# Where a hybrid transformer block opens the buffers of its second weight pair, and in which order the quarters of its output projection run

## The chip, the cores and the metric

The kernel runs on one core of one Trainium2 chip. The metric is the device time of one execution in microseconds (us); lower is better. Five engines run beside each other, each with its own instruction queue: TensorE (PE in the profile, its weight loads are PEld), VectorE (DVE), ScalarE (ACT), GpSimd (POOL) and SyncE (SP), which here only issues DMA loads.

## The reference

One layer for 256 tokens of width 2048, all in float32. The part that this case is about is the end of the first half and the start of the second:

```
h  = x + concat(att, u) @ w_out            # w_out: 2048 x 2048
hn = rms_norm(h, norm2_g)
a  = hn @ w_gate ; bu = hn @ w_up          # 2048 x 5632 each
h  = h + (silu(a) * bu) @ w_down           # 5632 x 2048
```

Ahead of it stand the input projection, a differential attention of 4 heads (whose output is `att`) and a causal convolution with layer norm (whose output is `u`).

## The kernel before, in words

**Precision.** Every float32 operand is split into a rounded half `hi` and a rest `lo`. A product of two split operands takes three matmuls (hi·hi, lo·hi, hi·lo). A weight chunk is loaded raw by SP, rounded to `hi` by ACT (L351) and its rest is taken by DVE (L360, `wlo<-raw,whi`). For some chunks, those written with a capital letter in `ORDER`, ACT writes −raw (L354) and POOL adds the raw weights by an accumulating DMA (L355) in place of DVE's subtraction.

**w_out.** Its 2048 columns go in four quarters of 512 (n = 0, 1, 2, 3). A chunk is two rows of 128 by 512 columns, 12 matmuls. Quarters 0, 1 and 2 go side by side: rows 0–3 of each, rows 4–5 of each, rows 6–7 of each, then rows 8–15 of each (4 chunks a quarter); quarter 3 then runs alone with all its 8 chunks. The text counts chunks back from the end of w_out: quarter 3 is chunks −8 to −1, the last four chunks of the quarter before it are −12 to −9, the ones before those −16 to −13; the very first chunk of w_out is −32. Accumulators lie in PSUM: a pair of banks of the pool `acc` (4 banks), but quarter 2 takes a pair of the pool `aux` (4 banks), which also serves every transpose and the attention's small products.

**What follows a quarter.** `out_done(n)` adds the accumulators to the residual (DVE, L874, two instructions, one for each 128 tokens), sends `h` to `out`, scales `h` (ACT, L883), transposes it on PE in two groups (L891, tile `ps_h`) and evacuates each group: quarters 0 and 2 into `hn` (ACT, L895); quarters 1 and 3 into a `hi` (ACT, L899) and a `lo` (DVE, L901). After quarter 2 it starts `make_forms`, which builds seven combinations of the blocks of `hn` (for a Strassen-like product with 7 multiplications) as hi (`fhi`, ACT L1009–L1011 and L1020) and lo (`flo`, DVE L1017, L1018, L1022), from sums by DVE (L1007, L1008, L1013, L1014).

**The second half** goes in 11 column blocks of gate and up. A block has 12 units: four `s` (a pair of rows from both matrices at once, 7 products of 3 matmuls each, Q1, Q6, Q7, Q5, Q2, Q4, Q3 in this order in the first), and eight plain chunks of gate (`g`) or up (`u`). A string gives the order; block 0 has one of its own. The weights of an `s` unit come as one load of 1 MB (`wb`); DVE makes sums of it (L1041–L1043, the "sums"), ACT rounds it (L1050, L1054, L1055, tile `wh`), and DVE takes the rests (L1059, L1060, tile `wl`); rounding and rests together are called its split below. `wh` and `wl` exist twice (`ffn["w", 0]` and `ffn["w", 1]`), for even and odd `s` units. The first set is opened after quarter 0 of w_out; the second by `open_second`, at the end of `out_done(3)`, when the whole group of pools of the first half (`h`, attention outputs, small vectors) is closed. Products Q1, Q6, Q7, Q5 take the four `acc` banks, Q2, Q4, Q3 and an eighth sum QX the four `aux` banks. At the last `s` unit of a block DVE runs six `bank_sums` (L1188–L1193), which free the banks for the next block.

**Who issues when.** The program text is emitted by one Python loop over chunks (`run_chunks`); each engine executes what it is given in that order, and waits in that order. Before it emits the matmuls of chunk t, the loop emits what looks ahead: in w_out the rest of chunk t+2 and the rounding of chunk t+3; from two chunks before the second half on, the rests of chunks up to t+3 (`LO_AHEAD`), the sums up to t+5, the roundings with a DMA up to t+5, other roundings up to t+4, loads up to t+9. Work that follows a quarter is a generator; each call of `resume()` lets each of them go one step on. `resume()` is called in the middle and at the end of a plain chunk, and in an `s` unit behind products 2, 4 and 6 and at the end. `start(done)` only queues a generator: its first step comes with the next `resume()`. A unit marked `prompt` calls `resume()` once more right behind its own last matmul.

A PSUM or SBUF tile that is asked for takes the place freed longest ago, and its first writer waits until the last reader of the old tile is done.

Of the kernel before, what the change touches and what calls it, by code (L numbers as in the profile page):

```python
# [13 lines left out]
F32 = mybir.dt.float32  # L14
# [67 lines left out]

ORDER = "sgGsgGsUUsUu"

FIRST = "sgguusGsGsUu"

Q1, Q6, Q7, Q5, Q2, Q4, Q3, QX = range(8)

PRODUCTS = ((Q1, 0, 5), (Q6, 5, 0), (Q7, 6, 1), (Q5, 4, 2), (Q2, 1, 6), (Q4, 2, 3), (Q3, 3, 4))
# [28 lines left out]
def tile_block(  # L118
# [9 lines left out]

    wp = ctx.enter_context(tc.tile_pool(name="wp", bufs=4))
    early = ctx.enter_context(tc.tile_pool(name="early", bufs=2))  # L130
    latestack, prestack = ExitStack(), ExitStack()
    vectors = latestack.enter_context(tc.tile_pool(name="vectors", bufs=1, side="right"))
    late = latestack.enter_context(tc.tile_pool(name="late", bufs=1, side="right"))
    once = latestack.enter_context(tc.tile_pool(name="once", bufs=1, side="right"))
    small = latestack.enter_context(tc.tile_pool(name="small", bufs=4, side="right"))
    pre = prestack.enter_context(tc.tile_pool(name="pre", bufs=2))
    acc_ps = ctx.enter_context(tc.tile_pool(name="acc", bufs=4, space=PSUM))
    aux_ps = ctx.enter_context(tc.tile_pool(name="aux", bufs=AUX, space=PSUM))
# [5 lines left out]
    ident = const.tile([P, P], F32, tag="ident", name="ident")  # L144
    make_identity(nc, ident)
    arena = [const.tile([P, BLOCKS, P], F32R, tag=f"l{x}", name=f"l{x}") for x in ("hi", "lo")]
    neghalf = vectors.tile([P, 8], F32, tag="neghalf", name="neghalf")
    pool.memset(neghalf, -0.5)


# [4 lines left out]

    warm_up(WARM)

    cols = vectors.tile([P, NR], F32, tag="cols", name="cols")
    halves_of_x = [early.tile([P, HK, S], F32, tag="wb", name="xt") for _ in range(2)]

    def x_load(ks, queue):
# [2 lines left out]
        queue.dma_start(out=halves_of_x[i][:, k : k + n].rearrange("p k s -> p (k s)"),  # L164
                        in_=xt[:, NR + ks[0] * S : NR + (ks[0] + n) * S])

    head = late.tile([P, NK * N], F32, tag="lod", name="head", bufs=1)[:, : NR + S]
    act.dma_start(out=head, in_=xt[:, : NR + S])
    x_load(XPARTS[1], act)
    x_load(range(2, 4), act)  # L170
    pool.tensor_scalar(cols, head[:, :NR], 1.0, 0.0, ALU.mult, ALU.add)

    act.copy(small.tile([P, 8], F32, tag="rsq", name="first"), neghalf)

    def col(key, k):
        return cols[:, AT[key] + k : AT[key] + k + 1]
# [165 lines left out]
        sp.dma_start(out=c["raw"].rearrange("p k n -> p (k n)"), in_=src)  # L342

    def minus_chunk(c):
        c["lo"] = c["view"](late.tile([P, NK * N], F32R, tag="lod", name="lod", bufs=1))
        act.activation(c["lo"], c["raw"], AF.Copy, scale=-1.0)
        pool.dma_start(out=c["lo"].rearrange("p k n -> p (k n)"), in_=c["src"].bitcast(F32R), accum_op=ALU.add)

# [134 lines left out]
    def run_chunks():  # L483
        n = len(chunks)
        pair_at.extend(i for i, c in enumerate(chunks) if "sides" in c)
        two_at.extend(i for i, c in enumerate(chunks) if "kind" in c and "sides" not in c)
        at = dict(part=0, dma=0, sums=0, round=0, minus=0, raw=0)
        first = next(i for i, c in enumerate(chunks) if "kind" in c)

        def until(what, do, stop, only=lambda c: True, may=lambda i: True):  # L490
            while at[what] < min(n, stop) and may(at[what]):
                if only(chunks[at[what]]):
                    do(at[what])
                at[what] += 1

        for t in range(n):
            if t >= first - AHEAD:
                until("part", part_of, t + 1 + LO_AHEAD)
                until("raw", lambda i: round_raw(chunks[i]), t + 1 + RAW_AHEAD, lambda c: "sides" in c,
                      lambda i: i <= t or may_round_raw(t, i))  # L500
                ahead = SUMS_AHEAD if t >= first else 0
                until("sums", sums_of, t + 1 + ahead - ("sides" in chunks[t] and bool(chunks[t].get("prompt"))), may=may_sum)
                until("dma", round_of, t + 1 + DMA_AHEAD, lambda c: c["by_dma"])
                until("round", round_of, t + 1 + (HI_AHEAD if t >= first else LO_AHEAD))
                load_until(t + 1 + LOAD_AHEAD)
            else:
                if t < len(XPARTS):
                    until("part", part_of, t + 2)
                else:
                    until("part", part_of, t + 1 + AHEAD)  # L510
                    until("minus", minus_of, min(t + 1 + MINUS_AHEAD, first), lambda c: c.get("minus"))
                    until("round", round_of, min(t + 1 + ROUND_AHEAD, first))
            part_of(t)
            chunks[t]["multiply"](chunks[t])
            if chunks[t].get("prompt") and chunks[t]["done"]:
                resume()
        while running:
            resume()
# [99 lines left out]
    def conv_back(b):  # L618
# [19 lines left out]
            return  # L638
        yield

        act.activation(small.tile([P, 8], F32, tag="rsq", name="first"), neghalf, AF.Silu)
        mv = small.tile([P, NM, 2], F32, tag="mv", name="mv", bufs=1)
        for m in range(NM):
            dve.bn_aggr(mv[:, m, :], stats[m].rearrange("p a b -> p (a b)"))
# [11 lines left out]
        for b in range(2):  # L656
            for t in range(NB // 2):
                yield from room(1)
                pt = aux_ps.tile([P, 2, S], F32, tag="aux", name="ps_ln")
                for j in range(2):  # L660
                    i = 2 * t + j
                    for m in range(NM):
                        pe.transpose(pt[:, j, m * P : (m + 1) * P], ytok[m, b][:, i * P : (i + 1) * P], ident)
                for j in range(2):
                    ct = b * NB + 2 * t + j
                    z = pre.tile([P, N], F32, tag="va", name="z")[:, :S]
                    act.activation(z, pt[:, j, :], AF.Silu, bias=col("lb", ct), scale=col("lg", ct))
                    hi = late.tile([P, S], F32R, tag="mchi", name=f"mchi{ct}", bufs=NCT)
                    lo = late.tile([P, S], F32R, tag="mclo", name=f"mclo{ct}", bufs=NCT)
                    dve.tensor_copy(hi, z)  # L670
                    dve.tensor_tensor(lo, z, hi.bitcast(F32), ALU.subtract)
                    mixc[ct] = (hi, lo)
                spend(0.7)
                yield from lag(2)
# [132 lines left out]
    def attend_values(hd):  # L807
# [26 lines left out]
        for e in range(2):  # L834
            for m in range(NM):
                pe.transpose(pt[:, e, m * P : (m + 1) * P], atts[m][:, e * P : (e + 1) * P], ident)
        pairs = [lhs_pair("a", 2 * hd + e) if hd >= 2 else tuple(
            late.tile([P, S], F32R, tag=t, name=t, bufs=4) for t in ("mahi", "malo")) for e in range(2)]
        for e, (hi, _) in enumerate(pairs):
            act.activation(hi, pt[:, e, :], AF.Copy, scale=col("sg", e))  # L840
        for e, (hi, lo) in enumerate(pairs):
# [20 lines left out]

    def open_second():

        latestack.close()
        spare_lhs.append(ffn["wt"].tile([P, SPARE, 2, S], F32R, tag="ahi", name="ahi"))
        fp = ffn["sum"] = ffn["w", 1] = ctx.enter_context(tc.tile_pool(name="ffn1", bufs=1))
        spare_lhs.append(fp.tile([P, SPARE, 2, S], F32R, tag="alo", name="alo"))
        ffn["plain"].append([fp.tile([P, HK - NS, S], F32R, tag=x, name=x) for x in ("chi", "clo")])

    def out_done(n, ps):
        cs = slice(n * N, (n + 1) * N)
        for m in range(NM):
            dve.tensor_tensor(h[m][:, cs], h[m][:, cs], ps[m], ALU.add)  # L874
        for m in range(NM):
# [33 lines left out]
        if n == D // N - 1:  # L909
            yield  # L910
            for m in range(NM):
                ss = small.tile([P, 1], F32, tag="ssh", name="ssh")
                dve.tensor_reduce(ss, ss2[m], AX.X, ALU.add)
                rsqrt_mean(rest[m], ss, D, EPS)
                pool.tensor_tensor(rest[m], rest[m], rms1[:, m : m + 1], ALU.mult)
            open_second()
            yield from lag(2)
            at = slot[0] % (KD // 2) * 4 - 2 * 4
            for a, c in zip(arena, ffn["plain"][1]):
                act.copy(c, a[:, at : at + 8].rearrange("p (k m) c -> p k (m c)", m=NM))  # L920
            for k in REST:
                i, k_ = divmod(k, HK)
                plain[k] = tuple(c[:, k_ - NS] for c in ffn["plain"][i])
# [145 lines left out]
    def multiply_pair(c):  # L1069
# [4 lines left out]
        for n, (q, f, w) in enumerate(products):  # L1074
# [3 lines left out]
            pe.matmul(ps, flo[:, f, p, :], c["hi"][:, w], start=False, stop=False)  # L1078
            pe.matmul(ps, fhi[:, f, p, :], c["lo"][:, w], start=False, stop=bool(last))  # L1079
            if n == 0 and c["done"]:  # L1080
                halfway["w1"] = ffn["sum"].tile([P, N], F32, tag="sum0", name="sum0")
                act.copy(halfway["w1"], ps)
            if n in (1, 3, 5):
# [180 lines left out]
        block("w_in", VC + b * N, range(KD), fx, lambda ps, b=b: v_done(b, ps))  # L1264
    for ks, first, last in ((range(0, 4), True, False), (range(4, 6), False, False), (range(6, 8), False, False),
                            (range(8, 16), False, True)):
        for n in range(3):
            block("w_out", n * N, ks, fm, (lambda ps, n=n: out_done(n, ps)) if last else None,
                  bkey=("o", n), first=first, last=last, spare=n == 2)
    block("w_out", 3 * N, range(16), fm, lambda ps: out_done(3, ps))  # L1270
    for m in range(NM):
        chunks[RAW_BUFS + m]["raw_tag"] = f"v{m}"
    for i, c in enumerate(chunks[len(XPARTS) : -12]):
# [2 lines left out]
    j0 = 0  # L1276
    for g, nb in enumerate(FGROUPS):
        for j in range(j0, j0 + nb):
            gate_up_block(j, FIRST if j == 0 else ORDER)
        for n in range(0, D // N, 2):  # L1280
            down_block(g, n)
        j0 += nb
# [46 lines left out]
```

## Time and profile before

| | |
|---|---|
| median of 3 runs | 1045.86 us (1045.74 to 1046.52) |
| the profiled execution | 1046.47 us, of which the span from first to last instruction is 1044.6 us |
| granted TensorE clock in it | 0.995 of full speed |
| busy share of the span | PE 98%, DVE 85%, ACT 68%, POOL 15% |
| where things lie | w_out's first chunk at about 241 us; its last matmuls at 338; block 0 of the second half 339 to 391; then ten more blocks and the down projections |

A timeline row reads: start in us, duration in us, engine, line, operation, tile written `<-` tiles read, shape, count of merged instructions, and in brackets how long the engine had been idle and what ended that. Durations of back-to-back matmuls overlap (a row says 0.39, their starts are 0.23 apart). A row of a table by stretches gives, for each engine, its busy time in the stretch and the count of its instructions, then the granted clock, the busy share of the DMA engines and GB/s. A row of waits gives total, times, longest.

### The profile page before, as it was taken

The numbers are of one execution on the slowest core, as the hardware profiler recorded it, in microseconds if no ns is written. First come the engines' busy times: TensorE is split into PE (matmuls) and PEld (weight loads), VectorE is DVE, ScalarE is ACT, GpSimd is POOL, SyncE is SP. The second block draws the span as 40 slices with busy tenths as digits, with TensorE's granted clock in tenths as the row PEclk, the third lists the DMA queues.
The fourth block names the chain that finished last, engine by engine and source line by source line (L and its number), as shares of the span: only waits on it lengthen the run. The fifth ranks groups of instructions, "written<-read, shape, count | busy, mean of one in ns | idle before, by whom it ended". The sixth has DMA issues, their size and how long they took to land. (4 is left out here: it accounts for less than half of the span.)

```text
span 1044.6 us, 13138 instructions
## 1 busy us (share of the span) xinstructions
PE 1027.8 (98%) x4621; PEld 847.4 (81%) x4621; DVE 891.6 (85%) x1121; ACT 707.6 (68%) x939; POOL 159.1 (15%) x205
## 2 busy tenths in 40 slices
PE   9999999999999798999999999999999999999998
PEld 7888888888888587888888888888888888888887
DVE  6699889897657599999999888999898897998984
ACT  7754667767766477687666666876766566767761
POOL 0140322311100111011012120110100221001121
PEclk9999999999999899999999999999999999999999
DMA  9968675665657398897989997988979999889896
GB/s 360 320 196 247 217 217 175 201 194 182 193 190 262 121 303 237 267 311 229 304 237 257 303 267 249 317 250 275 272 233 291 273 264 324 239 258 301 237 255 134
DMA packets 65346, 260.15 MB, mean 249 GB/s; under 512 B 7296, under 2 KB 8576, under 8 KB 56832
## 3 DMA queue, kind: packets, MB, share of 16 engines
q1 hardware_dynamic: 47648, 202.13, 52.9%
q0 software_dynamic: 17200, 56.63, 29.1%
q8 instruction: 36, 0.59, 0.2%
q10 hardware_dynamic: 432, 0.55, 0.2%
q14 instruction: 30, 0.25, 0.1%
HBM read 250.90 MB, written 8.39 MB: 248 GB/s over the span
## 5 line engine op out<-in xcount | busy, mean ns | idle before, releaser
L351 ACT CAST whi<-raw 128x1024 fp32r<-128x1024 f32 (+1 forms) x246 | 253.6, 1041 | 49.2 <-PE acc L391 31.8
L360 DVE TENSOR_TENSOR wlo<-raw,whi 128x1024 fp32r<-128x1024 f32 (+1 forms) x154 | 185.2, 1211 | 42.4 <-ACT whi L351 39.0
L1059 DVE TENSOR_TENSOR wl<-wb,wh 128x2048 fp32r<-128x2048 f32 x66 | 151.1, 2289 | 43.0 <-ACT wh L1054 42.6
L1050 ACT CAST wh<-wb 128x1536 fp32r<-128x1536 f32 x66 | 97.9, 1483 | 125.4 <-issue 65.8
L355 POOL DMA_DIRECT2D wlo<-in_wts_dram x78 | 68.7, 881 | 533.4 <-ACT wlo L354 409.7
L390 PE MATMUL acc<-whi,lhi 128*128 128x512 f32 x352 | 139.3, 396 | 0.2 <-ACT whi L351 0.2
L391 PE MATMUL acc<-whi,llo 128*128 128x512 f32 x352 | 137.6, 391 | 0.0
L1077 PE MATMUL q<-wh,fhi 128*128 128x512 f32 x308 | 122.0, 396 | 8.9 <-DVE h L874 6.1
L1079 PE MATMUL q<-wl,fhi 128*128 128x512 f32 x308 | 121.2, 393 | 1.4 <-DVE wl L1059 0.7
L1078 PE MATMUL q<-wh,flo 128*128 128x512 f32 x308 | 121.0, 393 | 0.0
L1060 DVE TENSOR_TENSOR wl<-wt,wh 128x1536 fp32r<-128x1536 f32 x66 | 115.7, 1752 | 0.0
L604 DVE SCALAR_TENSOR_TENSOR y<-upad,cw,y 128x256 f32<-128x256 f32 x240 | 100.8, 487 | 3.4 <-ACT y L597 3.4
L1055 ACT CAST wh<-wt 128x1536 fp32r<-128x1536 f32 x66 | 97.6, 1479 | 0.0
L1104 PE MATMUL q<-wlo,chi 128*128 128x512 f32 x336 | 91.3, 394 | 0.0
L1099 PE MATMUL q<-whi,chi 128*128 128x512 f32 x336 | 90.0, 390 | 0.0
L1099 PE MATMUL q<-whi,clo 128*128 128x512 f32 x336 | 89.9, 389 | 0.0
L396 PE MATMUL acc<-wlo,lhi 128*128 128x512 f32 x304 | 83.5, 395 | 0.6 <-DVE wlo L360 0.6
L354 ACT ACTIVATE wlo<-raw 128x1024 fp32r<-128x1024 f32 x78 | 82.3, 1055 | 0.0
L1041 DVE TENSOR_TENSOR wt<-wb 128x1024 f32<-128x1024 f32 x66 | 80.6, 1221 | 1.2 <-DMA wb<-in_wts_dram 0.7
L390 PEld LDWEIGHTS acc<-whi,lhi 128*128 128x128 f32 x352 | 66.4, 189 | 14.2 <-ACT whi L351 0.6
L391 PEld LDWEIGHTS acc<-whi,llo 128*128 128x128 f32 x352 | 66.4, 189 | 13.6
L1077 PEld LDWEIGHTS q<-wh,fhi 128*128 128x128 f32 x308 | 58.4, 190 | 22.5 <-DVE h L874 6.4
(221 smaller groups left out, 1792.8 us busy)
## 6 DMA issues: line engine op xcount, KB each, us to landing
raw<-in_wts_dram SPq DMA_DIRECT2D x242, 512.0 KB, 6.9
wb<-in_wts_dram SPq DMA_DIRECT2D x66, 1024.0 KB, 7.1
wlo<-in_wts_dram POOLq DMA_DIRECT2D x78, 512.0 KB, 9.3
lod<-in_wts_dram POOLq DMA_DIRECT2D x14, 512.0 KB, 6.1
out_dram<-sum POOLq DMA_DIRECT2D x22, 256.0 KB, 6.0
h<-in_x_dram SPq DMA_DIRECT2D x4, 512.0 KB, 8.9
out_dram<-h POOLq DMA_DIRECT2D x8, 256.0 KB, 3.5
xt<-in_xt_dram SPq DMA_DIRECT2D x6, 256.0 KB, 6.7
```

The costliest lines, as they stand in the source:

```text
L351: act.copy(c["hi"], c["raw"])
L360: dve.tensor_tensor(c["lo"], c["raw"], c["hi"].bitcast(F32), ALU.subtract)
L390: pe.matmul(ps[m], xhi[:, ms], hi[:, j, :], start=c["first"] and j == 0, stop=False)
L391: pe.matmul(ps[m], xlo[:, ms], hi[:, j, :], start=False, stop=False)
L604: dve.scalar_tensor_tensor(y[:, ct, :], src, wk, y[:, ct, :], ALU.mult, ALU.add)
L1050: act.copy(c["hi"][:, 4:], c["b"][:, 1:])
L1059: dve.tensor_tensor(c["lo"][:, 3:], c["b"], c["hi"][:, 3:].bitcast(F32), ALU.subtract)
L1060: dve.tensor_tensor(c["lo"][:, :3], c["t"], c["hi"][:, :3].bitcast(F32), ALU.subtract)
L1077: pe.matmul(ps, fhi[:, f, p, :], c["hi"][:, w], start=bool(first), stop=False)
L1078: pe.matmul(ps, flo[:, f, p, :], c["hi"][:, w], start=False, stop=False)
L1079: pe.matmul(ps, fhi[:, f, p, :], c["lo"][:, w], start=False, stop=bool(last))
L1099: pe.matmul(ps, plain[i][e][:, ms], hi[:, i, ns], stop=False, start=i == e == 0 and bool(c["first"].get(qs[m])))
```

## The change

Four things are moved.

- The pools on the right side of SBUF are regrouped. What w_out's matmuls read (attention and convolution outputs, and one weight buffer) goes into a pool `mix`, which is closed in the first step of `out_done(3)`; in its place `wh` and `wl` of the second set open there. The rest of the old group is closed where everything was closed before (now `open_third`).
- The last chunk of w_out is marked `prompt`, so the first step of `out_done(3)` is emitted right behind w_out's last matmul. In the two chunks ahead of the second half, rests are taken for one unit beyond t in place of three.
- Block 0 takes the order of the other blocks, `sgGsgGsUUsUu`, in place of `sgguusGsGsUu`. Its second `s` unit is then unit 3, not unit 5, and it has three plain chunks by DVE in place of five.
- w_out's first three quarters go 0, 2, 1 in each round, so quarter 2 ends with chunk −13 and quarter 1 with chunk −9.

The copy of two tiles at the end of `out_done(3)` comes ten steps later in place of two, and a unit that needs the pool of sums waits in the loop until it is open. A vector of constants is widened from 8 to 32 columns.

```
-FIRST = "sgguusGsGsUu"
...
-    latestack, prestack = ExitStack(), ExitStack()
-    vectors = latestack.enter_context(tc.tile_pool(name="vectors", bufs=1, side="right"))
+    latestack, mixstack, prestack = ExitStack(), ExitStack(), ExitStack()
...
+    mix = mixstack.enter_context(tc.tile_pool(name="mix", bufs=1, side="right"))
...
-                until("part", part_of, t + 1 + LO_AHEAD)
+                until("part", part_of, t + 1 + (LO_AHEAD if t >= first else 1))
...
-                    hi = late.tile([P, S], F32R, tag="mchi", name=f"mchi{ct}", bufs=NCT)
+                    hi = mix.tile([P, S], F32R, tag="mchi", name=f"mchi{ct}", bufs=NCT)
...
     def open_second():
 
+        mixstack.close()
+        ffn["w", 1] = ctx.enter_context(tc.tile_pool(name="ffn1", bufs=1))
+        for x in ("wh", "wl"):
+            ffn["w", 1].tile([P, 7, N], F32R, tag=x, name=x)
+
+    def open_third():
+
         latestack.close()
         spare_lhs.append(ffn["wt"].tile([P, SPARE, 2, S], F32R, tag="ahi", name="ahi"))
-        fp = ffn["sum"] = ffn["w", 1] = ctx.enter_context(tc.tile_pool(name="ffn1", bufs=1))
+        fp = ffn["sum"] = ctx.enter_context(tc.tile_pool(name="ffn2", bufs=1))
...
     def out_done(n, ps):
         cs = slice(n * N, (n + 1) * N)
+        if n == D // N - 1:
+            open_second()
...
-            open_second()
-            yield from lag(2)
+            open_third()
+            yield from lag(10)
...
+                while "sum" not in ffn:
+                    resume()
                 halfway["w1"] = ffn["sum"].tile([P, N], F32, tag="sum0", name="sum0")
...
-        for n in range(3):
+        for n in (0, 2, 1):
             block("w_out", n * N, ks, fm, (lambda ps, n=n: out_done(n, ps)) if last else None,
                   bkey=("o", n), first=first, last=last, spare=n == 2)
     block("w_out", 3 * N, range(16), fm, lambda ps: out_done(3, ps))
+    chunks[-1]["prompt"] = True
...
-            gate_up_block(j, FIRST if j == 0 else ORDER)
+            gate_up_block(j, ORDER)
```

More of the change, by code (lines that the diff above doesn't have):

```diff
@@ L146, in tile_block @@
     arena = [const.tile([P, BLOCKS, P], F32R, tag=f"l{x}", name=f"l{x}") for x in ("hi", "lo")]
-    neghalf = vectors.tile([P, 8], F32, tag="neghalf", name="neghalf")
+    neghalf = once.tile([P, 32], F32, tag="neghalf", name="neghalf")
     pool.memset(neghalf, -0.5)
@@ L156, in tile_block @@
     warm_up(WARM)
-    cols = vectors.tile([P, NR], F32, tag="cols", name="cols")
+    cols = once.tile([P, NR], F32, tag="cols", name="cols")
     halves_of_x = [early.tile([P, HK, S], F32, tag="wb", name="xt") for _ in range(2)]
@@ L165, in x_load @@
                         in_=xt[:, NR + ks[0] * S : NR + (ks[0] + n) * S])
-    head = late.tile([P, NK * N], F32, tag="lod", name="head", bufs=1)[:, : NR + S]
+    head = mix.tile([P, NK * N], F32, tag="lod", name="head", bufs=1)[:, : NR + S]
     act.dma_start(out=head, in_=xt[:, : NR + S])
@@ L171, in tile_block @@
     pool.tensor_scalar(cols, head[:, :NR], 1.0, 0.0, ALU.mult, ALU.add)
-    act.copy(small.tile([P, 8], F32, tag="rsq", name="first"), neghalf)
+    act.copy(small.tile([P, 8], F32, tag="rsq", name="first"), neghalf[:, :8])
     def col(key, k):
@@ L344, in minus_chunk @@
     def minus_chunk(c):
-        c["lo"] = c["view"](late.tile([P, NK * N], F32R, tag="lod", name="lod", bufs=1))
+        c["lo"] = c["view"](mix.tile([P, NK * N], F32R, tag="lod", name="lod", bufs=1))
         act.activation(c["lo"], c["raw"], AF.Copy, scale=-1.0)
@@ L639, in conv_back @@
         yield
-        act.activation(small.tile([P, 8], F32, tag="rsq", name="first"), neghalf, AF.Silu)
+        act.activation(small.tile([P, 8], F32, tag="rsq", name="first"), neghalf[:, :8], AF.Silu)
         mv = small.tile([P, NM, 2], F32, tag="mv", name="mv", bufs=1)
@@ L667, in conv_back @@
                     act.activation(z, pt[:, j, :], AF.Silu, bias=col("lb", ct), scale=col("lg", ct))
-                    hi = late.tile([P, S], F32R, tag="mchi", name=f"mchi{ct}", bufs=NCT)
-                    lo = late.tile([P, S], F32R, tag="mclo", name=f"mclo{ct}", bufs=NCT)
+                    hi = mix.tile([P, S], F32R, tag="mchi", name=f"mchi{ct}", bufs=NCT)
+                    lo = mix.tile([P, S], F32R, tag="mclo", name=f"mclo{ct}", bufs=NCT)
                     dve.tensor_copy(hi, z)
@@ L837, in attend_values @@
         pairs = [lhs_pair("a", 2 * hd + e) if hd >= 2 else tuple(
-            late.tile([P, S], F32R, tag=t, name=t, bufs=4) for t in ("mahi", "malo")) for e in range(2)]
+            mix.tile([P, S], F32R, tag=t, name=t, bufs=4) for t in ("mahi", "malo")) for e in range(2)]
         for e, (hi, _) in enumerate(pairs):
```

## The prediction

> **What bounds the kernel now.** I read the page's busy shares first, then PE's waits, then the table by stretches of 5 us where they fall.
>
> ```profile
> PE 1027.8 (98%) x4621; PEld 847.4 (81%) x4621; DVE 891.6 (85%) x1121; ACT 707.6 (68%) x939; POOL 159.1 (15%) x205
> ...
> PE q L1077 <- DVE h L874: 6.1, 1, 6.1
> PE q L1077 <- DVE sum L1188: 2.7, 1, 2.7
> ...
> PE q L1079 <- DVE wl L1059: 0.7, 1, 0.7
> PE q L1079 <- DVE wl L1060: 0.7, 1, 0.7
> ...
> 345.00:350.00 5.00, 2.24 (x5) 1.82 (x6) 3.23 (x5) 1.34 (x2) 1.09 (x2) 0.50 0.89 356
> ...
> 395.00:400.00 5.00, 5.00 (x14) 3.46 (x15) 4.90 (x9) 2.34 (x4) 0.00 (x0) 0.66 0.78 207
> ```
>
> PE is busy for 98% of the span, so only its losses are to be won, and they sit in one place: the start of the second half. Two waits there for DVE, of 6.1 and 2.7 us, and behind each a stretch at a granted clock of 0.50 and 0.66.
>
> ```profile
> 338.89 0.39 PE L1077 MATMUL q<-wh,fhi 128*128 128x512 f32 x1
> ...
> 347.76 0.79 PE L1077 MATMUL q<-wh,fhi 128*128 128x512 f32 x1 [6.09 <-DVE h L874]
> ...
> 352.79 0.60 PE L891 MATMUL ps_h<-ident,scaled 128*128 128x128 f32 x4
> 353.47 0.47 PE L1077 MATMUL q<-wh,fhi 128*128 128x512 f32 x1
> ...
> 354.23 1.07 PE L1099 MATMUL q<-whi,chi 128*128 128x512 f32 x4
> ...
> 391.31 0.39 PE L1077 MATMUL q<-wh,fhi 128*128 128x512 f32 x1
> ...
> 400.94 1.07 PE L1099 MATMUL q<-whi,chi 128*128 128x512 f32 x4
> ...
> 437.95 0.39 PE L1077 MATMUL q<-wh,fhi 128*128 128x512 f32 x1
> ...
> 442.03 0.39 PE L1077 MATMUL q<-wh,fhi 128*128 128x512 f32 x1
> ```
>
> An undisturbed `s` unit: six products from 437.95 to 442.03, 0.68 each, so 7 take 4.76. The first `s` unit runs from 338.89 to 354.23, 15.34, with two groups of transposes inside (0.36 each, estimated from a 0.60 row whose instructions overlap): 9.9 lost. The first of block 1 takes 400.94 − 391.31 = 9.63: 4.9 lost, of which 2.7 is the wait and the rest the low clock. With 0.7 at block 0's second `s` unit, **the loss before is 15.5 us**.
>
> Why PE waited 6.1 us is read on DVE.
>
> ```profile
> 341.03 3.49 DVE L360 TENSOR_TENSOR wlo<-raw,whi 128x1024 fp32r<-128x1024 f32 x3
> 344.44 1.22 DVE L1041 TENSOR_TENSOR wt<-wb 128x1024 f32<-128x1024 f32 x1
> ...
> 347.02 1.28 DVE L874 TENSOR_TENSOR h<-h,acc 128x512 f32<-128x512 f32 x2
> 352.45 0.88 DVE L901 SCALAR_TENSOR_TENSOR llo<-ps_h,cols,lhi 128x256 fp32r<-128x256 f32 x2 [4.15 <-ACT lhi L899]
> ```
>
> Quarter 3's addition L874, which frees the banks for Q7 and Q5, stood behind three rests and the next pair's sums. The last row matters for what follows: Q3 (353.47) starts 0.68 after the transposes, not 0.36, and right behind L901's end (353.33). Q3 takes the `aux` bank freed longest ago, that of the first `ps_h`, and waits until L901 has read it.
>
> **The change part by part.** Times below are on the clock of before, to be read against its rows.
>
> *Prompt, and one unit of look-ahead.* L874 of quarter 3 is now emitted before unit 0's look-ahead, with no rests of `g` units ahead of it. It can run as soon as w_out's last matmul ends: the 6.1 us go. The wide constant and the dummy tiles cost nothing on a path; POOL, which fills the constant, is 15% busy.
>
> *Opening `mix`.* `wh` and `wl` are 2 × 7 × 512 × 4 B = 28 KB a partition; `mix` holds 4 KB + 8 × 2 KB + 4 × 2 KB = 28 KB, whose last reader is w_out's last matmul. So unit 3 can be rounded at once. Before, ACT waited for the vector work behind quarter 3, and DVE stood still meanwhile.
>
> *What is late next.* Unit 0's look-ahead reaches unit 3, now an `s` unit: before its own matmuls the loop emits `g`'s rest, sums and split of unit 3, and the roundings of units 4 and 5. Quarter 3's L899 and L901 come behind all of it, and Q3 waits for L901. The pieces:
>
> ```profile
> 316.64 1.34 ACT L883 ACTIVATE scaled<-h,rstd 128x512 f32<-128x512 f32 x2
> ...
> 338.41 3.88 ACT L351 CAST whi<-raw 128x1024 fp32r<-128x1024 f32 x4
> ...
> 351.58 0.84 ACT L899 ACTIVATE lhi<-ps_h,cols 128x256 fp32r<-128x256 f32 x2 [2.50 <-PE ps_h L891]
> ...
> 315.92 1.28 DVE L874 TENSOR_TENSOR h<-h,acc 128x512 f32<-128x512 f32 x2 [0.41 <-PE acc L396]
> 317.12 1.22 DVE L360 TENSOR_TENSOR wlo<-raw,whi 128x1024 fp32r<-128x1024 f32 x1
> ...
> 333.80 1.22 DVE L1041 TENSOR_TENSOR wt<-wb 128x1024 f32<-128x1024 f32 x1
> ...
> 337.15 2.29 DVE L1059 TENSOR_TENSOR wl<-wb,wh 128x2048 fp32r<-128x2048 f32 x1 [0.69 <-ACT wh L1054]
> 339.36 1.75 DVE L1060 TENSOR_TENSOR wl<-wt,wh 128x1536 fp32r<-128x1536 f32 x1
> ```
>
> From the end E of w_out: L874 at E − 0.25, 1.20 until the next DVE instruction (315.92 to 317.12); `g`'s rest 1.15; sums 2.66 (333.80 to 337.15 − 0.69): E + 4.76. ACT then needs 1.95 for L1054 and L1055 (336.46 to 338.41), 3 × 0.95 for two roundings and one negative (the row with x4), then L899; L901 follows 0.87 behind it (351.58 to 352.45) and takes 0.88. Sum: E + 4.76 + 1.95 + 2.85 + 0.87 + 0.88 = E + 11.3, and Q3 at E + 11.4. PE has until then Q1 and Q6 (1.36), the transposes (behind L883, which ends 2.06 after L874 starts, so 0.5 late), Q7, Q5, Q2, Q4 and the second transposes: E + 5.3. It waits about 6.1 us there, and as before the low clock behind it costs 1.9 (347.76 to 352.79 holds four products and a group of transposes, 3.1 undisturbed, and took 5.0). **Unit 0 loses 0.5 + 6.1 + 1.9 = 8.5.** Bounds: 0.5 if L901 were not waited for, 10.5 if a load holds ACT up by 2. Unit 2's weights are a load of
>
> ```profile
> raw<-in_wts_dram SPq DMA_DIRECT2D x242, 512.0 KB, 6.9
> ```
>
> 6.9 us; it can be issued at about 333 (a buffer freed by chunk −3's rest), so its rounding, now ahead of `g`'s on ACT, is done by 342. I take 8.5, since the steps are rows. POOL's adding DMA for it has until 359.
>
> *Order 0, 2, 1.* `make_forms` runs four chunks earlier, so that unit 0 is split before w_out ends and its two small waits go, but the rows below now meet the work behind quarter 1.
>
> ```profile
> 312.08 1.99 ACT L351 CAST whi<-raw 128x1024 fp32r<-128x1024 f32 x2
> 324.87 0.61 ACT L1009 CAST fhi<-hn 128x512 fp32r<-128x512 f32 x1
> ...
> 326.44 1.04 ACT L351 CAST whi<-raw 128x1024 fp32r<-128x1024 f32 x1
> 328.78 1.91 ACT L1020 CAST fhi<-sums 128x2048 fp32r<-128x2048 f32 x1
> ...
> 328.65 1.29 DVE L1017 TENSOR_TENSOR flo<-hn,fhi 128x512 fp32r<-128x512 f32 x2
> 329.86 0.68 DVE L1018 SCALAR_TENSOR_TENSOR flo<-hn,fhi 128x512 fp32r<-128x512 f32 x1
> 331.59 2.29 DVE L1022 TENSOR_TENSOR flo<-sums,fhi 128x2048 fp32r<-128x2048 f32 x1
> ...
> 318.89 0.60 PE L891 MATMUL ps_h<-ident,scaled 128*128 128x128 f32 x4
> ```
>
> ACT: rounding of −7 at 312.08 to 313.0, three casts 1.57 (324.87 to 326.44) to 314.6, rounding of −6 to 315.6. DVE: rest of −6 to 316.85, L1017 and L1018 1.8 to 318.65, and only then quarter 1's L874, 2.7 later than its slot (315.92). L883 ends at 320.7, and PE, which wants to transpose at 318.89, waits 1.9. L1020 (1.9) stands between L883 and L899 on ACT: L901 starts at 323.4. From there DVE has no gap: L901 0.8, rest 1.15, L901 0.8, L1022 2.2, rest 1.15, sums 2.66, rest 1.15, L1059 2.2, L1060 1.7, rest of −2 1.2: 338.4. PE wants that rest at 336.9 (second half of −2, already 1.9 late) and waits 1.5 more. After it come 0.9 and a chunk of 2.72: w_out ends at 342.0 in place of 338.9. **3.1 lost.** Bounds: 1.9 (the transposes alone) and 4.5 (the chain's steps each 0.1 longer).
>
> Quarter 2's two `aux` banks are also taken two chunks earlier, at −30, just behind the convolution's transposes:
>
> ```profile
> 249.87 1.46 PE L817 MATMUL ps_o<-v,qT 128*128 128x256 f32 x6
> ...
> 250.36 1.09 ACT L630 COPY upad<-ps_y 128x512 f32<-128x512 f32 x2
> ```
>
> With two banks held by quarter 2, head 2's `ps_o` needs a bank of `ps_y`, free when ACT's first copy ends at 250.9. **1.1 lost**; bounds 0 (another bank is free) and 1.6 (the second copy).
>
> *Block 0's order.* Unit 3's split is done at E + 9.3, well before PE asks for it; DVE is not idle while ACT waits, and has 2 rests fewer (2.4 us). I followed the units on: unit 9 ends 385.7, the next block's first pair is split at 383 and its second one's sums done at 387.2, so L1188 runs there. Block 1's second product is at 391.8. That has 4 us of slack, as one block later, where L1188 starts at 434.06 and the unit at 437.95:
>
> ```profile
> 434.06 0.68 DVE L1188 TENSOR_TENSOR sum<-q,sum 128x512 f32<-128x512 f32 x1
> ```
>
> So the 2.7 wait and its low clock, 4.9, go. The later copy (L920, 2.1 us of ACT) falls between units 4 and 5, hidden by 5 us between unit 6's split and its use.
>
> **The sum.** After: 1.1 + 3.1 + 8.5 = 12.7 lost; before: 15.5. Gain 2.8: 1046.47 − 2.8 = 1043.7 against the profiled execution (span 1044.6 and 1.9 around it), which is 0.6 above the median; against the median **1043.1**.
>
> [...] The stretch 395–400 shows clock 0.66 behind a wait of 2.7 us. [...]
>
> **The rivals.** *Clock falls in w_out too.* For it: 2.7 us sufficed. Against: the 0.7 waits brought nothing. Each fall costs 1.9; of the first 1.5 goes into the later DVE wait, the second counts in full: +2.3, 1045.4. Chance 0.15.
>
> *The wait at block 1 stays* (the slower one). DVE's 85% is near 98% in this stretch; if unit 9's split and the two pairs of the next block slip until L1188 ends after 392.5, the 2.7 wait returns with its clock, +4.9: 1048.0, slower. It decides once DVE is 4 us later than I have it, which the end of w_out moving to 342 makes thinkable; PE moves with it, which speaks against. Chance 0.13.
>
> *Q3 does not wait for L901*, as another bank comes free. Then 6.1 + 1.9 less: 1035.1. The row at 353.47 speaks against it. Chance 0.07.
>
> **How the numbers follow.** My forecast has 0.55 and its own range 1040.5 to 1044.8; 0.10 is for what I have not seen. A measurement tells 0.2% (2.1 us) from no change. Faster, under 1043.8: two thirds of the forecast (0.42), the bank rival (0.07), 0.07 of the others: 0.56. Same: the upper end of the forecast (0.13), most of the clock rival (0.12), part of the slower one: 0.31. Slower, above 1047.9: 0.13. The range takes forecast, clock rival and half of the slower one: from 1038.5 (no wait for `ps_o`, w_out and Q3 1.7 shorter each) to 1048.0.
>
> **What would show it.** L874 of quarter 3 within 0.3 us of w_out's end; L901 behind L1060 and Q3 behind it with a wait of 5 to 7; a wait of about 2 for L883 at quarter 1's transposes and of 1 to 2 for L360 at −2; 1 us at head 2's `ps_o`; no wait for L1188. The prediction fails if one of the first two waits is absent (faster) or the last remains (slower).

## The result, and the profile after

The changed kernel takes 1043.9 us (median of 14 runs, 1042.6 to 1044.9); the kernel before took 1046.5 beside it (14 runs, 1045.3 to 1047.4). The ratio is 0.9977, 95% interval 0.9968 to 0.9985: 2.4 us faster by the ratio, where the prediction had 2.8. The profiled execution has a span of 1043.1 us (before 1044.6).

Lines of the changed kernel have other numbers. Those used below: L388 (first matmul of a w_out chunk, before L390), L394 and L358 (matmul of a rest in w_out, rest by DVE; before L396, L360), L815 (`ps_o`, L817), L881 (addition of a quarter, L874), L890 (`scaled`, L883), L898 (transposes, L891), L906 and L908 (evacuation by ACT and DVE, L899 and L901), L1048–L1050 (sums), L1057 to L1062 (rounding by ACT), L1066 and L1067 (rests of an `s` unit), L1084 (first matmul of a product, L1077), L1108 and L1113 (plain chunk; rest's matmul in it), L1197 and L1200 (`bank_sums`).

The page's first line after, then PE's waits:

```profile
PE 1027.0 (98%) x4621; PEld 846.4 (81%) x4621; DVE 889.3 (85%) x1119; ACT 709.3 (68%) x941; POOL 162.3 (16%) x207
```

```profile
PE q L1084 <- DVE llo L908: 5.8, 1, 5.8
PE ps_h L898 <- ACT scaled L890: 1.6, 3, 1.0
PE acc L394 <- DVE wlo L358: 1.4, 2, 0.9
...
PE ps_o L815 <- ACT upad L628: 0.7, 1, 0.7
```

Both waits of before are gone: 6.1 us for quarter 3's addition and 2.7 us for `bank_sums` in block 1. In their place stand one of 5.8 us for quarter 3's `llo`, and three kinds of short ones that the change brought with it. PE's timeline after has them in place:

```profile
248.18 0.48 PE L388 MATMUL acc<-whi,mahi 128*128 128x512 f32 x1
...
251.24 1.56 PE L815 MATMUL ps_o<-v,qT 128*128 128x256 f32 x6 [0.73 <-ACT upad L628]
...
253.56 0.39 PE L388 MATMUL acc<-whi,mahi 128*128 128x512 f32 x1
...
324.43 0.60 PE L898 MATMUL ps_h<-ident,scaled 128*128 128x128 f32 x4
...
339.61 1.20 PE L394 MATMUL acc<-wlo,mchi 128*128 128x512 f32 x4 [0.95 <-DVE wlo L358]
...
343.38 0.39 PE L1084 MATMUL q<-wh,fhi 128*128 128x512 f32 x1
...
354.78 0.76 PE L1084 MATMUL q<-wh,fhi 128*128 128x512 f32 x1 [5.78 <-DVE llo L908]
...
360.97 1.09 PE L1108 MATMUL q<-whi,chi 128*128 128x512 f32 x4
...
394.32 0.39 PE L1084 MATMUL q<-wh,fhi 128*128 128x512 f32 x1
...
399.08 1.07 PE L1108 MATMUL q<-whi,chi 128*128 128x512 f32 x4
```

The same places before, where the prediction did not show them:

```profile
247.96 0.48 PE L390 MATMUL acc<-whi,mahi 128*128 128x512 f32 x1
...
252.08 0.39 PE L390 MATMUL acc<-whi,mahi 128*128 128x512 f32 x1
...
321.18 0.60 PE L891 MATMUL ps_h<-ident,scaled 128*128 128x128 f32 x4
```

Chunk −30 takes 5.38 us (248.18 to 253.56) where it took 4.12: **1.26** for `ps_o`. w_out ends at 343.38 in place of 338.89, 4.49 later, of which 0.22 was there before chunk −30 and 1.26 is `ps_o`: **3.01** for the order of the quarters. Of that, 1.77 was reached at the second group of quarter 1's transposes (3.25 later than 321.18, less the 1.48 from above), and 1.24 came with the rest of chunk −2. Units 0 and 1 of the second half take 17.59 (343.38 to 360.97); undisturbed they are 8.20 (seven products 4.76, two groups of transposes 0.72, a chunk 2.72): **9.4** lost. Block 1's first unit takes 4.76 (394.32 to 399.08), the undisturbed time to the hundredth. The sum is 13.7 lost where before had 15.5, a gain of 1.8 in this execution. In another execution of the same kernel, of span 1041.1 us, w_out took as long but units 0 and 1 took 16.29 (342.67 to 358.96); there the sum is 12.4 and the gain 3.1. The 2.4 by the ratio lies between.

DVE behind the end of w_out in the changed kernel, and then ACT:

```profile
343.12 1.28 DVE L881 TENSOR_TENSOR h<-h,acc 128x512 f32<-128x512 f32 x2 [2.43 <-PE acc L394]
...
348.82 2.29 DVE L1066 TENSOR_TENSOR wl<-wb,wh 128x2048 fp32r<-128x2048 f32 x1 [0.69 <-ACT wh L1061]
351.03 1.75 DVE L1067 TENSOR_TENSOR wl<-wt,wh 128x1536 fp32r<-128x1536 f32 x1
353.76 1.66 DVE L908 SCALAR_TENSOR_TENSOR llo<-ps_h,cols,lhi 128x256 fp32r<-128x256 f32 x4 [0.98 <-ACT lhi L906]
```

```profile
350.06 1.04 ACT L349 CAST whi<-raw 128x1024 fp32r<-128x1024 f32 x1
...
352.90 1.56 ACT L906 ACTIVATE lhi<-ps_h,cols 128x256 fp32r<-128x256 f32 x4
```

With E = 343.38: the addition at E − 0.26, unit 3's split finished at E + 9.4, `lhi` only behind the roundings that the look-ahead put ahead of it, `llo` last, Q3 at E + 11.40. The order of units has its part in this: with unit 3 an `s` unit, the second pair lies within unit 0's look-ahead, and with its buffers open it can be split there.

### The profile page after: what moved, and what is told of

It reads as the page before. It is cut to its first block, busy times and chain, and to the rows that moved or that the text cites. A ratio compares the mean times of both kernels' runs of the same rounds, so it can differ in the third digit from the quotient of the medians.

```text
span 1043.1 us, 13145 instructions
## 1 busy us (share of the span) xinstructions
PE 1027.0 (98%) x4621; PEld 846.4 (81%) x4621; DVE 889.3 (85%) x1119; ACT 709.3 (68%) x941; POOL 162.3 (16%) x207
## 4 chain that ended last, share of the span: by engine, by line
PE 76%; DVE 13%; ACT 3%; DMA 3%; POOL 2%; issue 2%; SPq 0%; ACTq 0%; DVEq 0%
PE q L1108 22%; PE q L1113 11%; PE q L1084 10%; PE q L1085 10%; PE q L1086 10%; DVE y L602 5%; DVE wlo L358 4%; PE acc L394 4%; PE acc L388 4%; PE acc L389 4%; DMA raw<-in_wts_dram 1%; ACT whi L349 1%; PE ps_a L939 1%; DMA lamv<-in_vecs_dram 1%; POOL rsq L224 1%
## 5 line engine op out<-in xcount | busy, mean ns | idle before, releaser
L358 DVE TENSOR_TENSOR wlo<-raw,whi 128x1024 fp32r<-128x1024 f32 (+1 forms) x152 | 182.7, 1209 | 41.7 <-ACT whi L349 38.5
L1066 DVE TENSOR_TENSOR wl<-wb,wh 128x2048 fp32r<-128x2048 f32 x66 | 151.0, 2288 | 45.1 <-ACT wh L1061 44.7
L1057 ACT CAST wh<-wb 128x1536 fp32r<-128x1536 f32 x66 | 97.9, 1483 | 132.7 <-issue 72.8
L388 PE MATMUL acc<-whi,lhi 128*128 128x512 f32 x352 | 139.1, 395 | 0.6 <-ACT whi L349 0.5
L1084 PE MATMUL q<-wh,fhi 128*128 128x512 f32 x308 | 120.6, 391 | 5.8 <-DVE llo L908 5.8
L1067 DVE TENSOR_TENSOR wl<-wt,wh 128x1536 fp32r<-128x1536 f32 x66 | 115.6, 1752 | 0.0
L1062 ACT CAST wh<-wt 128x1536 fp32r<-128x1536 f32 x66 | 97.6, 1479 | 0.0
L1113 PE MATMUL q<-wlo,chi 128*128 128x512 f32 x336 | 91.8, 395 | 0.0
L1108 PE MATMUL q<-whi,chi 128*128 128x512 f32 x336 | 90.8, 392 | 0.0
L1108 PE MATMUL q<-whi,clo 128*128 128x512 f32 x336 | 90.8, 392 | 0.0
L352 ACT ACTIVATE wlo<-raw 128x1024 fp32r<-128x1024 f32 x80 | 84.4, 1055 | 0.3 <-PE q L1113 0.3
L394 PE MATMUL acc<-wlo,lhi 128*128 128x512 f32 x304 | 83.5, 395 | 0.5 <-DVE wlo L358 0.5
L1048 DVE TENSOR_TENSOR wt<-wb 128x1024 f32<-128x1024 f32 x66 | 80.5, 1220 | 1.1 <-DMA wb<-in_wts_dram 0.5
L388 PEld LDWEIGHTS acc<-whi,lhi 128*128 128x128 f32 x352 | 66.2, 188 | 15.3 <-ACT whi L349 1.8
L1108 PEld LDWEIGHTS q<-whi,chi 128*128 128x128 f32 x336 | 63.6, 189 | 13.6
```

Of the source, the lines that this page charges most:

```text
L358: dve.tensor_tensor(c["lo"], c["raw"], c["hi"].bitcast(F32), ALU.subtract)
L388: pe.matmul(ps[m], xhi[:, ms], hi[:, j, :], start=c["first"] and j == 0, stop=False)
L394: pe.matmul(ps[m], xhi[:, ms], lo[:, j, :], start=False, stop=c["last"] and j == nk - 1)
L1066: dve.tensor_tensor(c["lo"][:, 3:], c["b"], c["hi"][:, 3:].bitcast(F32), ALU.subtract)
L1084: pe.matmul(ps, fhi[:, f, p, :], c["hi"][:, w], start=bool(first), stop=False)
L1108: pe.matmul(ps, plain[i][e][:, ms], hi[:, i, ns], stop=False, start=i == e == 0 and bool(c["first"].get(qs[m])))
```

## The experiments

All ratios are to the kernel before, measured beside the runs in question. "By the ratio" means a difference of ratios times 1046.

### Which part brings and which costs

**Quarters 0, 1, 2 again in the first three rounds, 0, 2, 1 only in the last.** Quarter 2 takes its `aux` banks one chunk after quarter 1's, as before.

```
-        for n in (0, 2, 1):
+        for n in ((0, 2, 1) if last else (0, 1, 2)):
```

> The changed kernel, but in the first three rounds w_out's quarters go 0, 1, 2 again; only the last round, rows 8 to 15, keeps 0, 2, 1. Quarter 2 then takes its two aux banks at chunk -28 and not -30. My theory: the wait of head 2's ps_o for the copy of ps_y (0.7 us in the wait row, 1.3 us by the length of chunk -30) goes and nothing else moves: 1.3 us less than the changed kernel, 1042.6, ratio to before 0.9965. Rival: the delay was absorbed by later waits for DVE and ACT, so nothing is won: 1043.9, ratio 0.9977.

Measured: ratio 0.9967 (0.9954 to 0.9980). The `ps_o` wait is not in its list of waits any more, and chunk −30 takes 4.14 us again (247.79 to 251.93): that the early banks cause the 1.26 is shown by the trace. The 1 us of time is near the 1.3 expected, but its interval overlaps that of the changed kernel.

**Quarters 0, 1, 2 throughout.**

```
-        for n in (0, 2, 1):
+        for n in (0, 1, 2):
```

> The changed kernel with w_out's quarters in the order 0, 1, 2 in all rounds; all else stays changed. My theory: the order 0, 2, 1 costs w_out 4.3 us (1.3 at ps_o, 3.0 in its last chunks) and only buys that unit 0 is split early. With 0, 1, 2 w_out ends at about 338.9 again, but the rests of unit 0 end at 341.1, so L881 of quarter 3 starts there and Q3, 11.6 us behind it, starts at 352.7 where the changed kernel has 354.8: 2 us less, 1042.0, ratio 0.9957. Rival: the early make_forms carries the gain; without it unit 0 waits for its own split and for L881 as before, and 1 to 3 us are lost: 1045 to 1047, ratio 0.9985 to 1.0005.

Measured: ratio 0.9958 (0.9944 to 0.9971), as expected: the order 0, 2, 1 costs some 2 us here (its interval just overlaps that of the changed kernel). Q3 starts at 352.51, where 352.7 was expected and the changed kernel has 354.78. PE's waits in its profile, and DVE's row for quarter 3's addition:

```profile
PE q L1084 <- DVE llo L908: 5.8, 1, 5.8
PE ps_h L898 <- ACT scaled L890: 1.1, 2, 0.9
...
PE q L1086 <- DVE wl L1067: 0.7, 1, 0.7
PE acc L394 <- DVE wlo L358: 0.4, 1, 0.4
```

```profile
340.86 1.28 DVE L881 TENSOR_TENSOR h<-h,acc 128x512 f32<-128x512 f32 x2
```

The wait at `ps_o` is gone and the one for L358 down to a single one of 0.4, a small one for unit 0's split (L1067) is back, and Q3 waits as long as ever. The chain that it waits for begins with L881, which here stands behind unit 0's rests on DVE: 2.14 behind w_out's end (338.72), where the changed kernel has it 0.26 ahead. So of the 4.3 us that w_out wins, some 2 are lost again.

**Without the mark `prompt`.**

```
-    chunks[-1]["prompt"] = True
```

> The changed kernel without the prompt mark on w_out's last chunk. The first step of out_done(3) is then forced by unit 3's rounding, which needs the pool: L881 stands behind unit 1's rest and unit 3's sums on DVE; ACT's order is the same. My theory: DVE stood idle for 2.4 us ahead of L881 anyway and does the rest and the sums then; L881 starts 1.5 us later but unit 3's split, L908 and Q3 keep their times, so the mark is worth nothing as long as Q3 waits: 1043.9 within 0.5, ratio 0.9977. Rival: the mark is what removes the 6.1 us wait for L881, so without it 1.5 to 4 us come back: 1045.4 to 1048.

Measured: ratio 0.9969 (0.9958 to 0.9981); no loss. Its wait for `llo` is 4.1 in place of 5.8, and its waits for `scaled` are 2.8 in all in place of 1.6. While Q3 waits anyway, an earlier addition buys nothing.

### What Q3 waits for

**Look-ahead of unit 0 cut short.** Before unit 0's matmuls only unit 1's rest, unit 2's rounding and the sums of unit 3 are emitted, so quarter 3's L906 and L908 do not stand behind the split of unit 3 or the roundings of units 4 and 5. (For roundings the edit looks two units ahead, where the expectation says one.)

```
-    until("part", part_of, t + 1 + (LO_AHEAD if t >= first else 1))
+    until("part", part_of, t + 1 + (LO_AHEAD if t > first else 1))
...
-    until("dma", round_of, t + 1 + DMA_AHEAD, lambda c: c["by_dma"])
-    until("round", round_of, t + 1 + (HI_AHEAD if t >= first else LO_AHEAD))
+    until("dma", round_of, t + 1 + (DMA_AHEAD if t != first else 2), lambda c: c["by_dma"])
+    until("round", round_of, t + 1 + (HI_AHEAD if t > first else LO_AHEAD if t < first else 2))
```

> The changed kernel, but ahead of unit 0 the loop looks only one unit ahead for rests, one for roundings and one for roundings with a DMA; the sums of unit 3 stay where they are. So unit 3's rounding and rests, and the roundings of units 4 and 5, are emitted behind L906 and L908 of quarter 3. My theory: Q3's wait for L908 (5.8 us) and the low clock behind it (3.4 to 3.6 us) go, L908 of the first group ends about 349.0 where PE wants Q3 at 348.8; unit 3 is split by 354, in time for 355: 9 us less than the changed kernel, 1035.0, ratio 0.989. Rival 1: Q3 does not hang on L908 but on something that stays, so 5.8 us remain: 1043.9. Rival 2: unit 3's split is now late and PE waits there for the 5 us instead: 1039 to 1042.

Measured: 1037.2 us, ratio 0.9908 (0.9895 to 0.9922): 7.2 us under the changed kernel by the ratio. PE's row for Q3 has no wait, `llo` stands right behind the sums on DVE, and the clock stays full (1.00 in each stretch of 5 us from 335 to 370):

```profile
349.35 0.47 PE L1084 MATMUL q<-wh,fhi 128*128 128x512 f32 x1
```

```profile
348.34 1.65 DVE L908 SCALAR_TENSOR_TENSOR llo<-ps_h,cols,lhi 128x256 fp32r<-128x256 f32 x4
```

The 2 us missing to the expected 1035.0 are half explained by a new wait of 1.0 for the adding DMA of unit 5, which was issued later.

**The same in the order 0, 1, 2.**

> Both edits that helped: the shorter look-ahead at unit 0 and w_out's quarters in the order 0, 1, 2. My theory: their gains come from different places, so most of both is kept. Against the kernel with the short look-ahead alone (1037.2), w_out ends 4.3 us earlier, but unit 0 then waits 0.9 for its own rests and 1.1 for the scaled rows: 2.3 us less, 1034.9, ratio 0.9886. Rival: with 0, 1, 2 the L881 of quarter 3 stands behind unit 0's rests, and what w_out wins is lost there again: 1037, ratio 0.991.

Measured: 1036.0 us, ratio 0.9902 (0.9888 to 0.9915). Only 0.6 us less by the ratio, where 2.3 was expected, and not told apart from no difference: the 2 us that the order cost with Q3 waiting are not found in this ratio.

**In the order 0, 1, 2, with unit 5's negative copy left early** (the line with `DMA_AHEAD` as in the changed kernel).

> The same, but the rounding and the negative of unit 5 (the one with a DMA) stay ahead of unit 0, as in the changed kernel. In the kernel with the short look-ahead PE waited 1.0 us for that DMA at unit 5. My theory: ACT has room for these two (1.9 us) between the scaled rows and L906, because L908 waits for DVE's sums until 345.8 anyway, so the 1.0 goes and nothing else moves: 1033.9, ratio 0.9876. Rival: they delay L906 and with it Q3 by up to 1.9: 1035.5 to 1037, worse than without.

Measured: 1035.2 us, ratio 0.9892 (0.9879 to 0.9906), the fastest of all by a little: 11 us, 1.1%, under the kernel before. The DMA wait is gone, and the two instructions of unit 5 that stand ahead of L906 again do not make Q3 wait. That is still short of the 0.9876 expected: the profiled execution has a stretch of low clock in unit 0 (last section), and the one run that kept full clock took 1033.8, as the theory had it.

**The same in the order 0, 2, 1.**

> The changed kernel, order 0, 2, 1 kept, with unit 0's look-ahead cut to one unit for rests and two for roundings, the negative copy of unit 5 left early. Against the version with the adding DMA deferred too (1037.2, ratio 0.9908) the 1.0 us wait for that DMA goes: ratio 0.9898 (1036.2). Rival: the order 0, 2, 1 costs the full 2 us here as it does without the deferral, so 2 us over the same kernel in order 0, 1, 2 (0.9892): 0.9911.

Measured: 1035.6 us, ratio 0.9895 (0.9882 to 0.9908). As the theory had it, and the rival (the order costs the full 2 us) is just outside. By the medians, then, the order is worth nothing either way once Q3 does not wait. From the first product to unit 2, the order 0, 1, 2 takes 12.84 (338.94 to 351.78) and this one 9.19 (342.59 to 351.78), so 3.65 of the 4.3 that 0, 2, 1 loses in w_out (1.26 + 3.01) is lost in unit 0 otherwise.

But 1.2 of the 3.65 is the low clock of that execution. With the adding DMA deferred too, the order 0, 1, 2 kept full clock in its profiled execution (1.00 in each stretch from 335 to 400) and took 11.61 (338.81 to 350.42), only 2.4 more than 9.19. The run times agree. With the early copy, the order 0, 1, 2 took 1035.2 to 1035.6 in three runs with a mean clock of 0.998, and 1033.8 in one with 1.000; this order took 1035.2 to 1035.7 in four runs, all with 1.000. With the adding DMA deferred too it is 1035.2 and 1035.6 at 1.000, 1036.5 and 1036.7 at 0.998, against 1037.1 to 1037.8 at 1.000. So where the clock holds, 0, 1, 2 is ahead by some 1.7 us (few runs), but five of its eight runs stand at 0.998.

What is left of waits around the change in the order 0, 2, 1:

```profile
PE ps_h L898 <- ACT scaled L890: 1.6, 3, 1.0
...
PE acc L394 <- DVE wlo L358: 1.3, 2, 0.9
PE ps_o L815 <- ACT upad L628: 0.7, 1, 0.7
```

**The last but one without `prompt`.**

> The same without the prompt mark. In the changed kernel the mark was worth nothing. My theory: there Q3's wait hid it; here nothing does, and L881 of quarter 3 stands 3.8 us longer behind unit 1's rest and unit 3's sums: PE waits 4 us for Q7's bank and runs at half clock behind it, Q3 comes 2.4 later, in all 3.5 to 5.5 us more than with the mark: 1037.5 to 1039.5, ratio 0.991 to 0.993. Rival: the mark does nothing anywhere: 1034.

Measured: 1042.1 us, ratio 0.9969 (0.9957 to 0.9981): 8 us more by the ratio, where 3.5 to 5.5 was expected. PE's timeline:

```profile
345.23 0.79 PE L1084 MATMUL q<-wh,fhi 128*128 128x512 f32 x1 [3.82 <-DVE h L881]
```

The wait of the kernel before is back, 3.8 us long. The rest of the 8 us was not expected; PE's list of waits has 3.1 us more there for two adding DMAs that came late in units behind it. So the mark is worth nothing while Q3 waits, and several us when it doesn't.

### What cured block 1

**Block 0's old order, `sgguusGsGsUu`, and all else of the change.**

```
-            gate_up_block(j, ORDER)
+            gate_up_block(j, ORDER if j else FIRST)
```

> The changed kernel with block 0's old order of units, sgguusGsGsUu. Unit 3 is then a u, and the second pair unit 5. My theory: L908 of quarter 3 stands behind three rests and the sums, not behind a split: Q3 starts at about 351.2 in place of 354.8, the clock falls for a shorter time, and L1197 at block 1 still comes in time, because it was the early opening of the buffers and not the order that cured that wait: 3.5 to 5 us less than the changed kernel, 1039 to 1040.5, ratio 0.993 to 0.9943. Rival: the order cured it; DVE has 2.4 us more to do in block 0 and the wait of 2.7 us at block 1 with its low clock (4.9 together) returns: 1043.5 to 1045.5.

Measured: 1043.6 us, ratio 0.9972 (0.9963 to 0.9982). My theory (1039 to 1040.5) failed: as fast as the changed kernel. The time lies in the rival's range, but not by its mechanism: block 1 has no wait of 2.7 us, only one of 0.4 (for L1200), and no low clock (1.00 in 390–395 and 395–400). Run again, with the changed kernel beside it:

> The changed kernel with block 0's old order, beside the changed kernel itself. If the waits of its trace are what counts, it is 2.2 us shorter at Q3 (a wait of 3.6 in place of 5.8) and 0.9 longer at block 1: 1.3 us under the changed kernel, ratio 0.9965. Rival: the shorter wait buys nothing because the low clock behind it lasts as long; then the same 0.9977.

> The changed kernel once more, beside the three others of this call. Ratio to the kernel before 0.9977, within 0.0008; Q3 waits about 5.8 us for the rest of quarter 3 (L908) and block 1 does not wait.

Measured: the old order 0.9972 (0.9962 to 0.9981), the changed kernel 0.9974 (0.9963 to 0.9985); 1.3 us apart was expected, 0.2 was found; the intervals, some 1 us to either side, do not rule the 1.3 out. DVE's timeline with the old order shows why Q3 still waited 3.6 us:

```profile
343.94 3.49 DVE L358 TENSOR_TENSOR wlo<-raw,whi 128x1024 fp32r<-128x1024 f32 x3
348.56 1.22 DVE L1048 TENSOR_TENSOR wt<-wb 128x1024 f32<-128x1024 f32 x1 [1.14 <-DMA wb<-in_wts_dram]
349.82 0.69 DVE L1049 TENSOR_TENSOR wt<-wb,wt 128x512 f32<-128x512 f32 x1
350.55 0.69 DVE L1050 TENSOR_TENSOR wb<-wt,wb 128x512 f32<-128x512 f32 x1
351.16 1.65 DVE L908 SCALAR_TENSOR_TENSOR llo<-ps_h,cols,lhi 128x256 fp32r<-128x256 f32 x4
```

The sums of the second pair, looked ahead from unit 0, stand ahead of L908, and they wait for a load.

**The old order and the look-ahead cut short.** Rests are held back here, the sums are not.

> Block 0's old order, with the look-ahead of unit 0 cut as in the deferred version (rests one unit, roundings and DMAs two), so that Q3 has nothing to wait for. Theory: the early opening alone removes most of the wait at block 1, the old order loses 0.9 us there: ratio 0.9917 (against 0.9908 with the new order). Rival: the new order is what cured block 1; then its wait of 2.7 us and the low clock return, 4.9 us: 0.9955.

Measured: 1043.2 us, ratio 0.9974 (0.9965 to 0.9983), neither 0.9917 nor 0.9955. DVE and PE show two separate things:

```profile
348.53 1.23 DVE L1048 TENSOR_TENSOR wt<-wb 128x1024 f32<-128x1024 f32 x1 [3.55 <-DMA wb<-in_wts_dram]
```

```profile
352.14 0.47 PE L1084 MATMUL q<-wh,fhi 128*128 128x512 f32 x1 [3.70 <-DVE llo L908]
...
390.57 0.39 PE L1084 MATMUL q<-wh,fhi 128*128 128x512 f32 x1
...
392.01 0.50 PE L1084 MATMUL q<-wh,fhi 128*128 128x512 f32 x1 [0.60 <-DVE sum L1197]
...
394.20 0.50 PE L1084 MATMUL q<-wh,fhi 128*128 128x512 f32 x1 [0.44 <-DVE sum L1200]
...
397.09 1.07 PE L1108 MATMUL q<-whi,chi 128*128 128x512 f32 x4
```

First, the load lands at 348.5 in this run as in the one above, so taking two rests out of DVE's way only made DVE wait 3.55 in place of 1.14, and Q3's wait is the same (3.7). My expectation had overlooked that the sums stand in the look-ahead too. Second, block 1's first unit takes 6.52 (390.57 to 397.09): 1.8 lost, and no low clock (1.00 in the same two stretches), where before lost 4.9. With the old order alone it lost 0.9 (5.67 against 4.76). So the rest of the change takes most of block 1's loss away, and the new order the remaining 0.9 to 1.8, with 4 us of slack on top. That in the rest of the change it is the early opening is argued, not shown: no run has the new order with the buffers opened late.

## Why the prediction was right

By its own steps:

- *Prompt.* L881 at E − 0.26, predicted E − 0.25; the 6.1 us wait went. Shown by the trace; that the mark is what does it, by the version without it in which Q3 did not wait.
- *What is late next.* Q3 at E + 11.40, predicted E + 11.4; wait 5.8, predicted 6.1. The cause is shown by the cut look-ahead: without unit 3's split (and the roundings behind it) ahead of L906 and L908, no wait, and 7.2 us less. The rival that Q3 does not wait for L908 is out.
- *Low clock behind it.* Predicted 1.9 as one value. What is left of units 0 and 1 beside the 8.20, the 5.8 and the 0.5 predicted for the transposes is 1.8 in one execution (16.29) and 3.1 in the other (17.59). The term was mis-sized as a constant; it has more than one value (last section). Which value an execution gets was not in the prediction, so how near the median came to the forecast is in part luck: with 1.8 the loss is 12.4, with 3.1 it is 13.7.
- *Order 0, 2, 1.* Transposes 1.77 late, predicted 1.9; the rest of −2 another 1.24, predicted 1.5; together 3.01, predicted 3.1. The rival that the clock falls in w_out too is out: the stretches with these waits, 320–325 and 335–340, stand at 1.00 (first table of the last section), with waits of 1.05 and 0.28 at the transposes and of 0.95 at −2. The sum counts no low clock behind waits of 1.9 and 1.5; no run shows that waits of that length keep the clock, and measured were these shorter ones. The last section has waits of 0.71, 0.85 and 0.28 behind which it fell.
- *`ps_o`.* 1.26, predicted 1.1.
- *Block 1.* No wait, L1197 at 389.90 for a product at 395.00, some 4.4 us of slack between its end and that product; predicted 4. The slower rival is out. What the prediction had not split is which part did it: mostly the rest of the change (the early opening, it is argued), and not the order of units alone.

```profile
389.90 0.68 DVE L1197 TENSOR_TENSOR sum<-q,sum 128x512 f32<-128x512 f32 x1
```

The prediction summed 12.7 lost; the two executions of the changed kernel give 13.7 and 12.4. Where the change's gain went is thereby named: 6.1 + 2.7 us of waits and their low clock were removed, and the look-ahead of unit 0 became a wait of 5.8 us, because the new order of units brought the next pair within its reach and the early opening let its split stand ahead of quarter 3's evacuation in DVE's and ACT's queues. (With the old order of units Q3 waited 3.6, for the sums.)

## What to carry to other kernels

When a buffer is opened earlier, look at what the emission loop will now put into the in-order queues ahead of work that somebody waits for: here the freed split took the place of the old wait, and holding it back by one unit brought the gain (some 10 to 11 us in place of 2.4). Price each part of a change behind the longest wait that remains, since a part that is worth nothing while another wait covers it (the mark) can be worth several us once that wait is gone, and one that costs 2 us beside it (the order of quarters) can cost less or nothing without it. And when a queue is to be cleared, list every kind of look-ahead in it: rests were held back in one experiment and the sums, which here waited 1.14 and 3.55 us for a load, were not.

## What the runs showed of the hardware

The low clock came in portions of some 3.4 us, as worked out below. A stretch that lies wholly in it stands at 0.50 (355 to 360 below), so a stretch of 5 us that stands at 0.87 has 0.13 × 5 × 2 = 1.3 us of it. The first table is the changed kernel's first profiled execution, the second its second, the third the fastest version (order 0, 1, 2, cut look-ahead, unit 5's copy left early):

```profile
320.00:325.00 5.00, 3.67 (x20) 2.66 (x19) 1.67 (x4) 4.20 (x6) 1.08 (x2) 1.00 0.48 184
...
335.00:340.00 5.00, 4.05 (x19) 3.04 (x18) 5.00 (x4) 3.62 (x5) 0.00 (x0) 1.00 0.81 315
...
350.00:355.00 5.00, 0.22 (x1) 0.25 (x2) 4.02 (x6) 5.00 (x10) 0.90 (x1) 0.87 1.06 423
355.00:360.00 5.00, 5.00 (x12) 3.88 (x13) 4.30 (x8) 0.94 (x4) 3.80 (x6) 0.50 1.00 267
360.00:365.00 5.00, 5.00 (x22) 4.07 (x21) 0.85 (x1) 4.73 (x5) 0.93 (x1) 0.95 0.48 127
```

```profile
350.00:355.00 5.00, 0.92 (x2) 0.83 (x3) 3.79 (x7) 4.97 (x11) 1.02 (x2) 0.86 1.04 412
355.00:360.00 5.00, 5.00 (x19) 3.99 (x18) 3.81 (x5) 1.89 (x4) 3.67 (x6) 0.80 1.03 298
```

```profile
340.00:345.00 5.00, 3.16 (x12) 1.96 (x11) 4.96 (x6) 3.21 (x5) 1.11 (x2) 0.88 0.95 313
345.00:350.00 5.00, 5.00 (x21) 4.01 (x20) 2.93 (x8) 3.68 (x10) 1.79 (x4) 0.78 1.03 314
```

(0.13 + 0.50 + 0.05) × 5 × 2 = 6.8 us at half clock; (0.14 + 0.20) × 5 × 2 = 3.4; (0.12 + 0.22) × 5 × 2 = 3.4. Before's stretch 395–400 at 0.66 gives 3.4 too, and the other seven profiled executions with a low clock 3.4 (three) or 6.8 to 6.9 (four). The same kernel, with the same wait of 5.8 us, had one portion in one execution and two in another, which is 1.3 us of time between the two and a good part of the 2.3 us by which its runs differ.

What had not been expected is how little idle time stood ahead of a fall. In before it was a wait of 2.7 us (0.66 in the stretch 395–400). In the last rows above it was three short waits, on PE's timeline:

```profile
341.22 0.50 PE L1086 MATMUL q<-wl,fhi 128*128 128x512 f32 x1 [0.71 <-DVE wl L1067]
...
342.57 0.33 PE L898 MATMUL ps_h<-ident,scaled 128*128 128x128 f32 x1 [0.85 <-ACT scaled L890]
...
343.18 0.55 PE L898 MATMUL ps_h<-ident,scaled 128*128 128x128 f32 x3 [0.28 <-ACT scaled L890]
```

They make 1.84 us. The version with the adding DMA deferred too had the same three (0.69, 0.86, 0.29) in the same place and kept full clock in its profiled execution; of its four runs two have a mean clock of 1.000 and two of 0.998. So the same kernel goes either way, and no run shows what decides it.
